# A fused Trainium2 layer: modulation products in four column groups, denser x loads, and the first two projected features moved beside the loads

## The chip, the cores and the metric

The kernel runs on one core of one Trainium2 chip. The metric is device time in microseconds (us); the runs shown are single executions, and the profile is one execution of its own.

## The reference

One layer of a hybrid model in fp32 on 1024 tokens and 256 context tokens of 2048 channels. What matters here is its beginning, an adaptive layer norm and the input projection:

```python
def _modulation(cond, w_ada, b_ada):
    m = jax.nn.silu(cond.astype(F32)) @ w_ada + b_ada
    return jnp.split(m, 3, axis=-1)
...
    shift, scale, gate = _modulation(c, w_ada, b_ada)
    shift_c, scale_c, gate_c = _modulation(c_ctx, w_ada, b_ada)
    h = _layernorm(x, ADALN_EPS) * (1.0 + scale[:, None]) + shift[:, None]
    hc = _layernorm(xc, ADALN_EPS) * (1.0 + scale_c) + shift_c
    s5_u, s5_g, pool_u, pool_g, rkv, rwkv_g, w_codes, a_codes = _split_in(h @ w_in)
    s5_uc, s5_gc, pool_uc, pool_gc, rkv_c, rwkv_gc, w_codes_c, a_codes_c = _split_in(hc @ w_in)
```

Behind it come an S5 scan, a pooling branch, an RWKV recurrence in two directions and an output projection with a last layer norm. `w_in` has 50 blocks of 128 columns, called features here; the last two, 48 and 49, are the codes `w_codes` and `a_codes`.

## The kernel before

`adaln` makes the modulated layer norm. The shift and the scale come from 128 pieces of `w_ada`, each 128 rows by 512 columns (256 KB), which SyncE's queue (SP) loads into a ring of `ARAWS` buffers `araw`; each piece is the moving operand of a product whose stationary operand has two columns, silu of `c` and of `c_ctx`. Sixteen products add up in PSUM (`ada`) to 512 columns of the shift or of the scale. `modulate` copies that row out on ScalarE, turns it into columns by four small products (`misc<-ident,row`), adds the bias on VectorE (`mod`), and after a shift and its scale makes four channel tiles of the activations: VectorE scales and shifts `xT`, ScalarE rounds it (`hi`), VectorE takes the rest (`lo`); the context's tiles go the same way on ScalarE and GpSimd (`hc_hi`, `hc_lo`). Two channel tiles are a slice, and there are eight.

`layernorm` takes a tile of 128 tokens (eight of x, two of the context, 1 MB each): statistics and normalization on VectorE, sixteen transpositions on TensorE, the copies to `xT` shared by ScalarE and VectorE. One x tile is loaded after every seventh piece.

`in_proj` projects feature by feature. `project` runs over the eight slices; of each, two halves of the rounded and rest parts of the weights (`whi`, `wlo`) meet `hi` and `lo` in three products, over 1024 tokens (`pm`, two matmuls) and 256 context tokens (`pc`). SP loads the weights (`wraw`, 128 KB). The order of features is 48, 49, 0 to 3, 24 and so on; 0 to 3 feed S5, and 24 is the first key feature.

TensorE's main stream is written in program order; everything beside it (norm, modulation, `vectors`, `in_parts`, `s5_setup`) is a generator in `Sched`, whose `tick` emits a step when a rough clock of the engines (`Clock`) says that it is due. Each engine and SP's queue then take their instructions in that emitted order. In `project`, as soon as slice 7 is made, `begin` frees the modulation's tiles and starts three jobs: `vectors` (five row vectors loaded into `e`, transposed, then the convolution's 72 rows), `in_parts` (18 rounds that cut `cutraw` into `cuthi`, `cutlo` and store them to `z_lora` or `z_cd`), and `s5_setup` (among others eight rounds of `s5crow`, each transposed on TensorE and stored to `s5c`). After each of the two codes ScalarE takes it out of PSUM into `e0` (one buffer) once `vectors` is over, and stores it to `z_cdraw`. Behind feature 24 `sched.drain()` emits all that is left of the jobs before the next feature.

Of the kernel before, what the change touches and what calls it, by code (L numbers as in the profile page):

```python
# [18 lines left out]
T = 1024  # L19
TC = 256  # L20
# [5 lines left out]
ARAWS = 7  # L26
LINES = 3
RING = 20
# [31 lines left out]
def shape_constants():  # L60
# [5 lines left out]
    c["k_heads"] = hs  # L66
    s = np.arange(64)[:, None]
# [27 lines left out]
class Pace:  # L95
    """Order of emission for engines that take their instructions in turn. It keeps a rough clock of each engine; a job
    says what its next step runs on, for how long, and when its operands are there, and the step is emitted once it
    holds up no engine. Times are in microseconds."""
# [12 lines left out]
    def clocked(self, t, work, share):  # L111
        """When the tensor engine ends what it begins at t: at half its clock after a tick in which it did little."""
# [33 lines left out]
    def offer(self, until):  # L146
        """Emits what is ready: matrix products up to that time, other work not far beyond it."""
# [42 lines left out]
class Slots:  # L190
    """Tiles that jobs take and give back."""
# [44 lines left out]
class Clock:  # L236
    """A rough clock of each engine, kept from the instructions as they are emitted. Times are in microseconds."""
# [9 lines left out]
    def note(self, eng, op, args, kw):  # L247
# [33 lines left out]
class Noted:  # L281
    """An engine, or all of them, whose instructions a clock takes note of."""
# [17 lines left out]
class Rings:  # L300
    """A pool whose tiles the clock takes for the next in the place of an earlier one."""
# [13 lines left out]
    def free(self, tag, bufs, n=1, own=()):  # L315
        """When the next n tiles of that name have been given up, as far as is known; never, while one is kept."""
# [15 lines left out]
class Watched:  # L332
    """A tile context with a clock."""
# [66 lines left out]
def beside(sched, *gens):  # L400
    """Runs gens at the same time, and ends with the last of them."""
# [16 lines left out]
def build(tc, A, out):  # L418
    """A: name -> AP of the inputs and the constants."""
    nc = tc.nc  # L420
    with ExitStack() as ctx:
# [7 lines left out]
        g.kx = scratch("z_kx", (RW, 3, NT))          # k, its unit vector, r  # L429
# [9 lines left out]
        g.cd = scratch("z_cd", (5, 128, 4, 256))         # of each direction the codes in two parts  # L439
# [28 lines left out]
def load_cols_in_steps(tc, A, g, pool, psum, specs, name, ps_tile=None, rows=None):  # L468
    """Vectors cut into rows of 128, turned so that each row is a column."""
# [22 lines left out]
def phase_ab(tc, A, g, const):  # L492
    nc = tc.nc
    with ExitStack() as ctx:
# [8 lines left out]
        with tc.tile_pool(name="araw", bufs=ARAWS) as raws:  # L503
            sched = adaln(tc, A, g, const, hb, psA, ap_, raws, hc_hi, hc_lo)
        g.hc_hi, g.hc_lo = hc_hi, hc_lo
        in_proj(tc, A, g, psA, sched, actx)


def adaln(tc, A, g, const, hb, psA, ap_, raws, hc_hi, hc_lo):
    """The modulated layer norm of both sequences, channels on the partitions, split in two for the products. The main  # L510
    stream is that of the modulation's own products."""
# [13 lines left out]
    def ada_load():  # L525
# [8 lines left out]
        [(rows_of(A["c"], 16), 16), (rows_of(A["c_ctx"], 16), 16), (rows_of(A["b_ada"], 48), 48)], "cv")  # L534
    ada_load()
    x_load()
    g.sil = sil = const.tile([128, 16, 2], FT, name="sil")
# [4 lines left out]
    mod = ap_.tile([128, 16, 2, 2], FT, name="mod")   # [k, shift|scale, c|c_ctx]  # L542
# [40 lines left out]
    def modulate(blk, part, ps):  # L583
        """A block of the modulation as columns; after its second half the block of the activations."""
        row = ap_.tile([2, 512], FT, name="row", tag="row")
        nc.scalar.activation(row, ps[0:2], AF.Copy)
        yield
        pt = psA.tile([128, 512], FT, name="misc", tag="misc", bufs=2)
        for i in range(4):
            nc.tensor.matmul(pt[:, 2 * i:2 * i + 2], row[0:2, i * 128:(i + 1) * 128], g.ident[0:2, 0:2], start=True, stop=True)  # L590
# [10 lines left out]
        while len(hi) < 2 * blk:  # L601
            yield
        for i in (2 * blk, 2 * blk + 1):
# [16 lines left out]

    for j in range(LINES):
# [2019 lines left out]
```

## Time and profile before

| what | value |
|---|---|
| runs | 3113.01, 3110.97, 3103.5 us; median 3110.97 |
| profiled execution | span 3105.6 us (its own time beside the span is not given) |
| TensorE busy | 2901.1 us, 93% |
| VectorE, ScalarE, GpSimd busy | 1992.7, 1024.8, 1030.4 us |
| DMA | 502.56 MB, mean 162 GB/s |

The span is that of one profiled execution, and is read beside the runs, not in their place. TensorE's busy share is a mean over all stages; the change lies in the first 240 us and at one place near 384 us.

### The profile page before, as it was taken

What the parts mean: (1) busy time and instruction counts of PE and PEld (TensorE: products, weight loads), DVE (VectorE), ACT (ScalarE), POOL (GpSimd) and SP (SyncE); (2) the same over time, 40 slices, a digit from 0 to 9 for tenths busy, and PEclk for the clock granted to TensorE, in tenths of its full rate; (3) what the DMA queues carried; (4) which work ended last, traced back from release to release, by engine and by line L of the source; (5) the groups of instructions that cost most, each with busy time, mean ns of one, the idle gap of its engine ahead of it and who ended that gap; (6) DMA issues with size and microseconds to landing.
All of it is one profiled execution on the core that took longest, in us unless ns stands there. A gap on an engine that the chain in (4) does not pass through costs nothing.

```text
span 3105.6 us, 55655 instructions
## 1 busy us (share of the span) xinstructions
PE 2901.1 (93%) x20080; PEld 2350.2 (76%) x20080; DVE 1992.7 (64%) x4464; ACT 1024.8 (33%) x2408; POOL 1030.4 (33%) x1414
## 2 busy tenths in 40 slices
PE   7989999999999999999899779999999999899976
PEld 2268787888888878788677478888888887788855
DVE  5547245545555458898886574766667765774668
ACT  1422223444444443322222223333234333333223
POOL 0103012233333335323541232434344343433516
PEclk9999999999999999999999879899899997996988
DMA  8835634445554555565344655566466665554664
GB/s 279 262 96 157 139 119 156 141 156 168 164 165 150 168 169 158 170 170 160 111 116 133 232 152 157 149 174 176 125 185 175 159 168 151 148 145 114 180 225 153
DMA packets 598828, 502.56 MB, mean 162 GB/s; under 512 B 205358, under 2 KB 519446, under 8 KB 595734
## 3 DMA queue, kind: packets, MB, share of 16 engines
q1 hardware_dynamic: 572792, 453.63, 50.1%
q0 software_dynamic: 6912, 24.12, 2.7%
q10 hardware_dynamic: 18848, 21.24, 2.0%
q8 instruction: 159, 2.61, 0.4%
q14 instruction: 117, 0.96, 0.1%
HBM read 343.77 MB, written 155.07 MB: 161 GB/s over the span
## 4 chain that ended last, share of the span: by engine, by line
PE 71%; DVE 15%; DMA 7%; issue 3%; SPq 2%; ACT 2%; POOL 1%; ACTq 0%; DVEq 0%; POOLq 0%
PE pm L293 28%; PE misc L293 6%; PE gp L1716 4%; PE pc L293 3%; PE ofacc L2371 3%; PE banky L1952 3%; PE ada L293 3%; PE banky L1949 3%; PE banku L1963 2%; PE ofacc L2372 2%; PE ofacc L2373 2%; DVE tmp L1843 2%; PE banky L1982 2%; PE misc L1901 2%; PE misc L1890 2%
## 5 line engine op out<-in xcount | busy, mean ns | idle before, releaser
L293 PE MATMUL pm<-hi,whi 128*128 128x512 f32 x1600 | 509.2, 400 | 7.1 <-ACT whi L293 7.1
L293 PE MATMUL pm<-lo,whi 128*128 128x512 f32 x1600 | 511.5, 401 | 0.0
L293 PE MATMUL pm<-hi,wlo 128*128 128x512 f32 x1600 | 509.0, 399 | 1.6 <-DVE wlo L293 1.6
L293 DVE TENSOR_TENSOR wlo<-wraw,whi 128x256 fp32r<-128x256 f32 x400 | 206.5, 525 | 373.5 <-ACT whi L293 356.5
L293 PEld LDWEIGHTS pm<-hi,whi 128*128 128x128 f32 x1600 | 275.4, 190 | 60.2 <-ACT whi L293 9.4
L293 PEld LDWEIGHTS pm<-hi,wlo 128*128 128x128 f32 x1600 | 274.4, 189 | 54.4 <-DVE wlo L293 2.8
L293 PEld LDWEIGHTS pm<-lo,whi 128*128 128x128 f32 x1600 | 274.0, 190 | 50.3 <-issue 1.8
L293 ACT ACTIVATE whi<-wraw 128x256 fp32r<-128x256 f32 x400 | 160.4, 413 | 400.9 <-DMA wraw<-in_w_in 252.6
L2371 PE MATMUL ofacc<-ofhi,ofyh 128*128 128x256 f32 x768 | 252.6, 329 | 24.3 <-DVE ofev L2388 10.2
L233 POOL TENSOR_TENSOR oflo<-ofw,ofhi 128x256 fp32r<-128x256 f32 x161 | 123.0, 765 | 426.4 <-ACT ofhi L227 308.5
L1989 DVE SCALAR_TENSOR_TENSOR ping<-ping,els,banku 64x64 f32<-64x64 f32 x480 | 134.1, 279 | 177.8 <-PE banku L1975 167.1
L2373 PE MATMUL ofacc<-oflo,ofyh 128*128 128x256 f32 x768 | 227.8, 297 | 1.6 <-POOL oflo L233 1.5
L2372 PE MATMUL ofacc<-ofhi,ofyl 128*128 128x256 f32 x768 | 228.0, 297 | 0.8 <-POOL ofyl L233 0.8
L2371 PEld LDWEIGHTS ofacc<-ofhi,ofyh 128*128 128x128 f32 x768 | 156.8, 204 | 39.1 <-issue 14.3
L1716 PE MATMUL gp<-spread,kq 128*128 128x128 f32 x1152 | 169.9, 295 | 15.5 <-DVE spread L229 6.7
L1716 PEld LDWEIGHTS gp<-spread,kq 128*128 128x128 f32 x1152 | 147.7, 202 | 24.8 <-DVE spread L229 7.0
L2373 PEld LDWEIGHTS ofacc<-oflo,ofyh 128*128 128x128 f32 x768 | 157.6, 205 | 2.7 <-POOL oflo L233 2.3
L2372 PEld LDWEIGHTS ofacc<-ofhi,ofyl 128*128 128x128 f32 x768 | 158.4, 206 | 1.1 <-POOL ofyl L233 1.1
L1843 DVE TENSOR_TENSOR tmp<-af,nn 128x31 f32<-128x31 f32 (+15 forms) x310 | 143.5, 463 | 14.2 <-DMA af<-flat 5.1
L1845 DVE TENSOR_TENSOR nn<-nn,tmp 128x31 f32<-128x31 f32 (+15 forms) x310 | 144.9, 468 | 10.7
L1956 ACT ACTIVATE rhs<-banky 64x256 f32<-64x256 f32 x128 | 48.1, 376 | 271.7 <-PE banky L1952 271.7
L293 ACT ACTIVATE th<-misc,rhalf 128x256 f32<-128x256 f32 x160 | 67.0, 470 | 209.3 <-PE misc L293 191.9
(513 smaller groups left out, 5975.3 us busy)
## 6 DMA issues: line engine op xcount, KB each, us to landing
wraw<-in_w_in SPq DMA_DIRECT2D x400, 128.0 KB, 2.4
z_kq<-kq SPq DMA_DIRECT2D x80, 512.0 KB, 3.9
kq<-z_kq SPq DMA_DIRECT2D x80, 512.0 KB, 4.5
araw<-in_w_ada SPq DMA_DIRECT2D x128, 256.0 KB, 5.0
ofw<-in_w_out SPq DMA_DIRECT2D x192, 128.0 KB, 3.2
part<-ofev SPq DMA_DIRECT2D x96, 256.0 KB, 2.5
cds<-z_cd POOLq DMA_DIRECT2D x40, 512.0 KB, 4.4
agraw<-in_w_ada SPq DMA_DIRECT2D x64, 256.0 KB, 3.0
```

Source lines behind the costliest of these rows:

```text
L233: (nc.vector if eng == "dve" else nc.gpsimd).tensor_tensor(out, a, b, op=op)
L293: r = x(*args, **kw)
L1716: nc.tensor.matmul(gp[:, i], seg.kb[:, i, :], qb[:, i].rearrange("p h t -> p (h t)"), start=True, stop=True)
L1843: nc.vector.tensor_tensor(tv, af[:, q, q + 1:].unsqueeze(2).to_broadcast([128, nt_, nj]), nn[:, q:q + 1, 0:nj].to_broadcast([128, nt_, nj] ...
L1845: nc.vector.tensor_tensor(nn[:, q + 1:, 0:nj], nn[:, q + 1:, 0:nj], tv, op=OP.subtract)
L1890: nc.tensor.matmul(pv[:, j], aq[64:96, c, h * 64 + 32:h * 64 + 64], n1[64:96, j], start=True, stop=True)
L1949: nc.tensor.matmul(yo, seg.qt[:, i], ch.s[d], start=(d == 0), stop=False, skip_group_check=True)
L1952: nc.tensor.matmul(yo[0:64, hs], seg.aq[0:64, i, hs], seg.uv[0:64, ch.uv[d], hs], start=False, stop=False, skip_group_check=True)
L1989: nc.vector.scalar_tensor_tensor(ch.s[d][hs, hs], ch.s[d][hs, hs], seg.el[hs, ch.c[d]:ch.c[d] + 1], b_u[hs, 2 + d, hs], op0=OP.mult, op1=O ...
L2371: nc.tensor.matmul(o, yh[:, sl], whi, start=(first and b == 0), stop=False, skip_group_check=True)
L2372: nc.tensor.matmul(o, yl[:, sl], whi, start=False, stop=False, skip_group_check=True)
L2373: nc.tensor.matmul(o, yh[:, sl], wlo, start=False, stop=last, skip_group_check=True)
```

## The change

Four things are changed in `adaln`, and `in_proj` is fitted to them; the removed docstrings and comments change nothing.

- The stationary operand `sil32` is 32 columns wide (30 of them zero). Products of four consecutive pieces go to PSUM partitions 0, 32, 64 and 96, so to four column groups of the array; `row` is copied out with all 128 partitions, and the turning product uses `fours`, which adds the four groups. `ARAWS` is 5 in the place of 7.
- An x tile is loaded after every second piece.
- In `modulate` the next channel's scale and shift stand ahead of the subtraction.
- Features 48 and 49 (`HEAD`) are projected in `adaln`, slice by slice, as soon as a slice is made: `head_units` holds both `pm` and both `pc` tiles, the weights come over GpSimd's queue into `wraw1`. `pass_time` puts their products where the clock expects the next four pieces to be on their way. `adaln` ends when all sixteen are done; only then `begin` starts the three jobs, and both codes are taken out ahead of feature 0.

```diff
-ARAWS = 7
+ARAWS = 5
+HEAD = (48, 49)
...
+                if out.shape[0] == 32:
+                    cost /= 4
...
+    sil = ap_.tile([128, 16, 32], FT, name="sil32")
+    nc.gpsimd.memset(sil, 0.0)
...
-        row = ap_.tile([2, 512], FT, name="row", tag="row")
-        nc.scalar.activation(row, ps[0:2], AF.Copy)
+        row = ap_.tile([128, 512], FT, name="row", tag="row")
+        nc.scalar.activation(row, ps, AF.Copy)
...
-            nc.tensor.matmul(pt[:, 2 * i:2 * i + 2], row[0:2, i * 128:(i + 1) * 128], g.ident[0:2, 0:2], start=True, stop=True)
+            nc.tensor.matmul(pt[:, 2 * i:2 * i + 2], row[:, i * 128:(i + 1) * 128], fours, start=True, stop=True)
...
-                x, xc = xT[i][:, j], xc_t[:, k]
-                nc.vector.tensor_scalar(x, x, mod[:, k, 1, 0:1], mod[:, k, 0, 0:1], op0=OP.mult, op1=OP.add)
+                xc = xc_t[:, k]
                 nc.scalar.activation(h_hi[:, j], x, AF.Copy)
+                x_next = shifted(k + 1) if k % 4 < 3 else None
                 nc.vector.tensor_tensor(h_lo[:, j], x, h_hi[:, j].bitcast(FT), op=OP.subtract)
+                x = x_next
...
+            nc.gpsimd.dma_start(raw, A["w_in"][0, s * 256:(s + 1) * 256, f * 128:(f + 1) * 128]
+                                .rearrange("(k p) n -> p k n", p=128))
...
+    def head_units():
+
+
+        for n, (s, f) in enumerate(heads):
+            while s not in made:
+                yield None
+            while len(parts) < min(n + 2, len(heads)):
+                w_split()
+            if f not in g.head:
+                g.head[f] = (psA.tile([128, T], FT, name="pm", tag="pm", bufs=2),
+                             psA.tile([128, TC], FT, name="pc", tag="acc", bufs=2))
...
+                    for half in range(2):
+                        nc.tensor.matmul(pm[:, half * 512:(half + 1) * 512], w[:, i, :],
+                                         hs[s][:, i, half * 512:(half + 1) * 512], **st)
+                    nc.tensor.matmul(pc, w[:, i, :], hcs[:, 2 * s + i, :], **st)
+                    yield 0.0
...
+    def pass_time(t):
+
+        clock = tc.clock
+        while True:
+            sched.tick()
+            now = clock.free["tensor"]
+            if now >= t - 0.3:
+                return
+            if not (raw_w and head_step()):
+                clock.free["tensor"] = min(now + 0.25, t)
...
-            if len(loaded) % 7 == 0 and len(x_t) < 10:
+            if len(loaded) % 2 == 0 and len(x_t) < 10:
                 x_load()
         if k == 0:
-            ps = psA.tile([128, 512], FT, name="ada", tag="acc", bufs=2)
-        nc.tensor.matmul(ps[0:2], sil[:, k, :], loaded[n], start=(k == 0), stop=(k == 15))
+            ps = psA.tile([128, 512], FT, name="ada", tag="misc", bufs=2)
+        if k % 4 == 0:
+            if len(normed) == 10 and not raw_w:
+                w_ahead()
+            pass_time(max(tc.clock.written[x.tensor.name][1] for x in loaded[n:n + 4]))
+        c = 32 * (k % 4)
+        nc.tensor.matmul(ps[c:c + 32], sil[:, k, :], loaded[n], start=(k < 4), stop=(k >= 12))
...
+        begin()
         for j, fn in enumerate((AF.Tanh, AF.Copy)):
-            pm, pc = project(48 + j, True)
+            pm, pc = g.head[HEAD[j]]
             while not made.vectors:
                 sched.wait()
```

**TensorE, end of the x transpositions.** `ada<-araw` are the modulation's products, `pm<-ident,x` half of an x tile's transpositions. Before, around the last tile:

```order
L293 MATMUL pm<-ident,x_664 128x128 x8
L293 MATMUL ada<-araw,sil 2x512 x2
L293 MATMUL pm<-ident,x_664 128x128 x8
L293 MATMUL ada<-araw,sil 2x512 x6
L293 MATMUL misc<-ident,row 128x2 x4
L293 MATMUL ada<-araw,sil 2x512 x18
L293 MATMUL misc<-ident,row 128x2 x4
L293 MATMUL ada<-araw,sil 2x512 x13
```

And of the change, with the first unit of feature 48 behind it:

```order
L297 MATMUL pm<-ident,x_373 128x128 x8
L297 MATMUL pm<-ident,x_365 128x128 x8
L297 MATMUL pm<-ident,x_373 128x128 x8
L297 MATMUL ada<-araw,sil_164 32x512 x4
L297 MATMUL misc<-fours,row 128x2 x4
L297 MATMUL ada<-araw,sil_164 32x512 x8
L297 MATMUL pm<-hi_695,whi_725 128x512 x2
L297 MATMUL pc<-hc_hi,whi_725 128x256
```

The last transpositions stood behind 61 pieces and now stand behind 28; the projection began behind all 128 and now begins behind 40.

**ScalarE, behind the last unit.** `e_1634` and `e_1638` are the two codes taken out of PSUM (one buffer), `whi` the split weights of feature 0. Of the change:

```order
L297 ACTIVATE whi_1488<-wraw_1433 128x256
L297 ACTIVATE cuthi<-cutraw 128x256
L297 ACT_TABLE_LOAD
L297 ACTIVATE e_1634<-pm 128x1024
L297 ACTIVATE e_1634<-pc 128x256
L297 DMA z_cdraw<-e_1634 128x1280
L297 ACTIVATE e_1638<-pm 128x1024
L297 ACTIVATE e_1638<-pc 128x256
L297 DMA z_cdraw<-e_1638 128x1280
L297 ACTIVATE whi<-wraw 128x256 x3
```

Before, eight splits of the next feature's weights and three of the cuts lay between the two codes; now nothing does, and the weights of feature 0 stand behind both.

**SP, the drain behind feature 24.** `s5crow` and `s5c` are rounds of S5's factors, `z_cd` and `cutraw` the codes' cuts. Before, from the last weights to the next:

```order
L293 DMA z_cd<-cuthi 64x256
L293 DMA z_cd<-cutlo 64x256
L293 DMA z_cd<-cuthi 64x256
L293 DMA z_cd<-cutlo 64x256
L293 DMA s5c<-s5cc 128x256
L293 DMA s5crow<-in_s_c_re 128x64
L293 DMA s5crow<-in_s_c_im 128x64
L293 DMA s5crow<-in_s_c_re 128x64
L293 DMA s5c<-s5cc 128x256
L293 DMA s5crow<-in_s_c_re 128x64
L293 DMA s5crow<-in_s_c_im 128x64
L293 DMA s5crow<-in_s_c_re 128x64
```

The first part of what stands there now:

```order
L297 DMA s5c<-s5cc 128x256
L297 DMA s5crow<-in_s_c_re 128x64
L297 DMA s5crow<-in_s_c_im 128x64
L297 DMA s5crow<-in_s_c_re 128x64
L297 DMA z_cd<-cuthi 64x256
L297 DMA z_cd<-cutlo 64x256
L297 DMA z_cd<-cuthi 64x256
L297 DMA z_cd<-cutlo 64x256
L297 DMA cutraw<-z_cdraw 128x256
L297 DMA s5c<-s5cc 128x256
L297 DMA s5crow<-in_s_c_re 128x64
L297 DMA s5crow<-in_s_c_im 128x64
```

The rest repeats it: `z_cd` four at a time stands there three times (before once), and 34 loads and stores go out ahead of the last `s5crow` (before 12). On TensorE `misc<-ident,s5crow` is there 14 times in a row and was 10 times.

## Rows read from the trace of the kernel before

**Rows 1.** The page: the span and its instructions.

```profile
span 3105.6 us, 55655 instructions
```

**Rows 2.** Windows: length (us), busy time by engine, granted clock, DMA share, GB/s.

```profile
0.00:167.00 167.00, 147.46 (x473) 46.09 (x473) 88.08 (x156) 46.39 (x97) 10.06 (x16) 0.97 0.79 265
...
120.00:140.00 20.00, 20.00 (x57) 5.02 (x55) 10.82 (x11) 10.46 (x17) 4.11 (x5) 1.00 0.89 292
```

**Rows 3.** The chain that ended last, first 300 us: start, length, work.

```profile
140.40 15.54 PE ada L293 x36
```

**Rows 4.** Groups by form, first 167 us: count | busy, mean ns | idle.

```profile
L293 PE MATMUL ada<-araw,sil 128*2 128x512 f32 x256 | 118.8, 611 | 2.7 <-DMA araw<-in_w_ada 2.7
...
L293 DVE BATCH_NORM_STATS2 bst<-x 128x6 f32<-128x512 f32 x40 | 24.7, 679 | 11.5 <-DMA x<-in_x 11.2 <-DMA x<-in_ctx 0.4
...
L293 DVE TENSOR_SCALAR x<-x,mv 128x2048 f32<-128x2048 f32 x10 | 13.5, 1346 | 0.4
...
L293 DVE TENSOR_TENSOR lo<-xT,hi 128x1024 fp32r<-128x1024 f32 x12 | 14.7, 1225 | 13.5 <-ACT hi L293 13.5
...
L293 DVE COPY xT<-pm 128x256 f32<-128x256 f32 x32 | 13.4, 424 | 20.0 <-ACT xT L293 20.0
...
L293 DVE BATCH_NORM_AGGREGATE mv<-bst 128x2 f32<-128x24 f32 x10 | 2.6, 264 | 0.3
```

**Rows 5.** Loads araw, issue to landing: all, then 120 to 167 us.

```profile
DMA to landing us min/median/max: 2.8/5.0/8.0
...
araw<-in_w_ada SPq DMA_DIRECT2D x45, 256.0 KB, 3.1
```

**Rows 6.** Timeline of PE near 1907 us: start, length, products.

```profile
1907.22 0.45 PE L1975 MATMUL banku<-uv,kbn 128*64 128x64 f32 x8
...
1907.51 0.63 PE L1982 MATMUL banky<-uv,ar 128*64 128x64 f32 x8
...
1908.07 0.68 PE L2040 MATMUL misc<-rhsc,aq 64*64 64x64 f32 x8
```

**Rows 7.** Timeline behind the last modulation product, 167 to 173 us.

```profile
167.41 0.59 ACT L293 ACTIVATE row<-ada 2x512 f32<-2x512 f32 x1 [13.01 <-PE ada L293]
...
172.22 0.81 DVE L293 TENSOR_SCALAR xT<-xT,mod 128x1024 f32<-128x1024 f32 x1
```

**Rows 8.** Timeline 188 to 200 us: the vectors' loads and transposition.

```profile
188.28 0.47 SPq L293 DMA_DIRECT2D heads<-in_k_heads  x1
...
190.40 0.29 SPq L293 DMA_DIRECT2D e<-in_rwkv_r_k  x1
...
192.90 0.32 PE L293 MATMUL misc<-ident,e 56*128 56x56 f32 x1 [7.48 <-DMA e<-in_rwkv_r_k]
```

**Rows 9.** Timeline: a step of products near 201 us, and the second feature's end.

```profile
201.09 0.63 PE L293 MATMUL pm<-hi,wlo 128*128 128x512 f32 x2
...
201.68 0.62 PE L293 MATMUL pm<-hi,whi 128*128 128x512 f32 x2
...
239.20 1.03 ACT L293 ACTIVATE e<-pm 128x1024 f32<-128x1024 f32 x1 [2.03 <-PE pm L293]
```

**Rows 10.** Timeline near 211 us, and z_cdraw's landing (last row).

```profile
211.10 1.03 ACT L293 ACTIVATE e<-pm 128x1024 f32<-128x1024 f32 x1 [6.03 <-PE pm L293]
...
212.43 0.35 ACTq L293 DMA_DIRECT2D z_cdraw<-e  x1
...
DMA to landing us min/median/max: 2.3/2.4/3.2
```

**Rows 11.** Timeline of the stretch behind the fifth feature, 383 to 390 us.

```profile
383.63 0.60 PE L293 MATMUL misc<-ident,s5crow 128*128 128x128 f32 x4
...
386.98 0.38 SPq L293 DMA_DIRECT2D s5crow<-in_s_c_re  x1
...
389.49 0.79 PE L293 MATMUL misc<-ident,s5crow 128*128 128x128 f32 x2 [1.16 <-DMA s5crow<-in_s_c_im]
...
389.94 1.20 PE L293 MATMUL pm<-hi,whi 128*128 128x512 f32 x2
```

More of the change, by code (lines that the diff above doesn't have):

```diff
@@ L66, in shape_constants @@
     c["k_heads"] = hs
+    c["k_fours"] = np.tile(np.eye(32, 2, dtype=np.float32), (4, 1))
     s = np.arange(64)[:, None]
@@ L502, in phase_ab, with adaln @@
         ap_ = actx.enter_context(tc.tile_pool(name="apool", bufs=1, side="right"))
[L503 to L504 removed]
         g.hc_hi, g.hc_lo = hc_hi, hc_lo
[L506 to L509 removed]
+        with tc.tile_pool(name="araw", bufs=ARAWS) as raws, ExitStack() as wctx:
+            sched = adaln(tc, A, g, const, hb, psA, ap_, raws, wctx, hc_hi, hc_lo)
+        assert not sched.q
+        actx.close()
+        in_proj(tc, A, g, psA, sched)
+def adaln(tc, A, g, const, hb, psA, ap_, raws, wctx, hc_hi, hc_lo):
     nc = tc.nc
@@ L602, in modulate, with shifted @@
             yield
+        def shifted(k):
+            x = xT[k // 2][:, k % 2]
+            nc.vector.tensor_scalar(x, x, mod[:, k, 1, 0:1], mod[:, k, 0, 0:1], op0=OP.mult, op1=OP.add)
+            return x
+        x = shifted(4 * blk)
         for i in (2 * blk, 2 * blk + 1):
@@ L619, in modulate, with w_ahead @@
                 yield
+    wp = wctx.enter_context(tc.tile_pool(name="wfirst", bufs=1))
+    heads = [(s, f) for s in range(8) for f in HEAD]
+    raw_w, parts, g.head = [], [], {}
+    def w_ahead():
+        while len(raw_w) < len(heads) and len(raw_w) < len(parts) + 2:
+            s, f = heads[len(raw_w)]
+            raw = wp.tile([128, 2, 128], FT, name="wraw1", tag="wraw1", bufs=2)
+            nc.gpsimd.dma_start(raw, A["w_in"][0, s * 256:(s + 1) * 256, f * 128:(f + 1) * 128]
+                                .rearrange("(k p) n -> p k n", p=128))
+            raw_w.append(raw)
@@ new lines, in w_split @@
+    def w_split():
+        w_ahead()
+        raw = raw_w[len(parts)]
+        whi = wp.tile([128, 2, 128], FR, name="whi1", tag="whi1", bufs=2)
+        wlo = wp.tile([128, 2, 128], FR, name="wlo1", tag="wlo1", bufs=2)
+        nc.scalar.activation(whi, raw, AF.Copy)
+        nc.vector.tensor_tensor(wlo, raw, whi.bitcast(FT), op=OP.subtract)
+        parts.append((whi, wlo))
+        w_ahead()
+    def head_units():
[7 more added lines that the diff above has]
+                             psA.tile([128, TC], FT, name="pc", tag="acc", bufs=2))
+            pm, pc = g.head[f]
+            whi, wlo = parts[n]
+            yield max(tc.clock.written[x.tensor.name][1] for x in (wlo, lo[s], hc_lo))
+            for i in range(2):
+                for m, (w, hs, hcs) in enumerate(((whi, hi, hc_hi), (whi, lo, hc_lo), (wlo, hi, hc_hi))):
+                    st = dict(start=(s == i == m == 0), stop=(s == 7 and i == 1 and m == 2))
+                    for half in range(2):
[3 more added lines that the diff above has]
+                    yield 0.0
@@ new lines, in adaln, with head_step @@
+    units = head_units()
+    ready = [None]
+    def head_step():
+        while ready[0] is None:
+            ready[0] = next(units, "end")
+            if ready[0] is None:
+                return False
+        if ready[0] == "end" or ready[0] > tc.clock.free["tensor"]:
+            return False
+        ready[0] = next(units, "end")
+        return True
+    def pass_time(t):
[7 more added lines that the diff above has]
+                clock.free["tensor"] = min(now + 0.25, t)
@@ L625, in adaln, with in_proj @@
             ada_load()
-            if len(loaded) % 7 == 0 and len(x_t) < 10:
+            if len(loaded) % 2 == 0 and len(x_t) < 10:
                 x_load()
         if k == 0:
-            ps = psA.tile([128, 512], FT, name="ada", tag="acc", bufs=2)
-        nc.tensor.matmul(ps[0:2], sil[:, k, :], loaded[n], start=(k == 0), stop=(k == 15))
+            ps = psA.tile([128, 512], FT, name="ada", tag="misc", bufs=2)
+        if k % 4 == 0:
+            if len(normed) == 10 and not raw_w:
+                w_ahead()
+            pass_time(max(tc.clock.written[x.tensor.name][1] for x in loaded[n:n + 4]))
+        c = 32 * (k % 4)
+        nc.tensor.matmul(ps[c:c + 32], sil[:, k, :], loaded[n], start=(k < 4), stop=(k >= 12))
         if k == 15:
             sched.add(modulate(blk, part, ps), 0)
+    while ready[0] != "end":
         sched.tick()
+        if not head_step() and ready[0] != "end":
+            if sched.q:
+                sched.wait()
+            else:
+                tc.clock.free["tensor"] = ready[0]
     return sched
-def in_proj(tc, A, g, psA, sched, actx):
+def in_proj(tc, A, g, psA, sched):
     nc = tc.nc
@@ L643, in in_proj @@
         kvs, kvts = ExitStack(), ExitStack()
-        feats = ([48, 49] + list(range(0, 4)) + [f for i in range(8) for f in (24 + i, 16 + i, 32 + i)] + list(range(8, 16)) + list(range(4, 8)) + list(range(40, 48)))
+        feats = (list(range(0, 4)) + [f for i in range(8) for f in (24 + i, 16 + i, 32 + i)] + list(range(8, 16)) + list(range(4, 8)) + list(range(40, 48)))
         todo = [(f, s) for f in feats for s in range(8)]
@@ L674, in project @@
             for s in range(8):
-                while s not in g.made:
-                    sched.wait()
-                if len(g.made) == 8 and not made.begun:
-                    begin()
                 whi, wlo = w_load(f, s)
@@ L695, in in_proj @@
         made.k = made.r = 0
-        made.busy = made.held = made.begun = made.vectors = False
+        made.busy = made.held = made.vectors = False
         def begin():
-            made.begun = True
-            actx.close()
             sched.add(vectors())
@@ L1148, in ada_gate @@
             yield raw,
[L1149 removed]
+            sc = g.sil[:, k:k + 1]
             if k == 0:
```

8 lines of the change are left out of this document (5 added, 3 removed).

## The prediction

> **What bounds the kernel now.** I read the windows first, then the chain that ended last, then groups by form, and last the timelines of the places that the change moves. The profiled span is 3105.6 us [rows 1]; no other time of that execution is given, and the median of the three runs shown, 3110.97 us, is 5.4 us above it. I work in differences and apply the sum to the median.
>
> The change touches the first 240 us and one place near 384 us. In the first 167 us the modulation's weights and x are loaded, and TensorE is busy for 147 of them; from 120 to 140 us it has no idle time at full clock while the DMA engines carry 292 GB/s [rows 2]. The chain there is nothing but modulation products, 36 in a row in 15.54 us [rows 3]. A record of that group counts twice per product (256 for 128 pieces, each a 256 KB slice of w_ada), so one piece takes 15.54/18 = 0.863 us [rows 3, 4]. Hence TensorE paces the end of the loads. Behind it codes 48 and 49 are projected, ending at about 239.1 us [rows 9]; a wait of 7.48 us for vectors lies between [rows 8].
>
> **Part 1, the column groups.** Four consecutive pieces now go to four groups of 32 columns. No row of before shows four groups. The nearest are two runs of eight small products: those that alternate between two column halves start 0.29 us before the next run, those that all lie in one half 0.56 us before it (1907.51 − 1907.22 and 1908.07 − 1907.51) [rows 6]. Two groups thus overlap almost wholly. Per four pieces the bounds are 3.45 us (no overlap), 1.73 (two at a time) and 0.86 (all four). I take 0.86 to 1.73, being nearest to that pair; either way TensorE is no longer the pace, so the choice does not enter the sum.
>
> The Trainium skill, "TensorEngine Tiling (Array Packing)", section Key Properties, states that a change of tiling mode drains TensorE, which speaks against groups of four between full-width products. Rows 6 pass from products on 128 rows and 64 columns to products on 64 rows and 64 columns, and the second run starts 0.07 us before the first one's modelled end: no hole of 0.1 us. Some 45 changes at that bound would be 4 us, an estimate, in slack beside the loads.
>
> What is late next is the load. There are now five buffers, not seven. A buffer's round is landing, wait, product: landing took 3.1 us in the undisturbed part, 2.8 at least, 5.0 in the middle of all [rows 5]. With 3.1 + about 1.0 (four nearly parallel products) + 0.15 for release, a round is 4.27 us, over five buffers 0.854 us per piece; by the lower bound 0.79, by the median 1.23. So the products become four times cheaper and the pace hardly changes. That is the first reason why the gain is small.
>
> **Part 2, x per two pieces.** All ten x tiles are then asked for by piece 16 instead of piece 56. The layer norm becomes VectorE's: per tile four statistics (4 × 0.679), an aggregate 0.264 and some 0.3 of small ones, the normalization 1.346, four copies (4 × 0.424), 6.3 us [rows 4]; 63 us for ten, from some 8 us on, with a few us for gaps: the last transpositions at about 75 us (72 to 84). In the order the last of them stand behind piece 28, and five more lie loaded.
>
> **Part 3, codes beside the loads.** Sixteen units (18 products, 6 steps of 0.59 us, 3.5 us) stand between pieces [rows 9]. After 75 us come four pieces, the second modulation row, eight pieces, the first slices' channels and the first weights, about 11 us (12 pieces less the five loaded, 7 × 0.854 = 6 us, and some 5 for row and first slice). Then 88 pieces and 12 units: 12 × 3.5 = 42 us of TensorE, and 88 × 0.854 = 75 us of loads, partly one beside the other, since in a unit only five buffers can fill. By the order a block of 32 pieces has four units, three of whose groups of four wait hidden, and 20 pieces that wait bare: 4 × 3.5 + 20 × 0.854 + about 4 = 35 us; two blocks and the last 24 pieces make 97 us (82 to 105). The last product ends at 75 + 11 + 97 = 183 us, 16 later than before. The head weights go over GpSimd's queue, which costs SP no issue; their 2 MB take 7 us of the loads' 290 GB/s [rows 2], inside the 97.
>
> **Part 4, the tail.** The last modulation row, its transposition and the sum took from 167.41 to 172.22 us, with other work between [rows 7]; 2.6 us when nothing stands between. Behind it slices 6 and 7 are made. VectorE's order now has the next channel's scaling ahead of the subtraction, so a channel costs VectorE's own two, 1.23 for the subtraction [rows 4] and 0.8 to 1.2 for the scaling [rows 7], about 2.3 us, with the rounding beside them; four units (14.2 us) then take 17.8 us, the wait for slice 6 included. The codes end at 183 + 20.4 = 203.5 us.
>
> **Part 5, what the codes' projection used to cover.** `begin` (vectors, factors, S5's setup) now stands behind the last unit. Its wait for vectors was 7.48 us bare already [rows 8]; the rest hid under 28 us of feature 48. Now: five vector loads issued in 2.4 us (188.28 to 190.69), landing 2.2 (to 192.90), so the first transposition is at +4.7 us [rows 8]; the convolution's load waits for it and for the copy out of PSUM (0.5), is issued (0.5), lands 2.2 later and is turned at +8.2; only then may ScalarE take the first code out (1.03 + 0.38 us), from +8.6 to +10.0; its store lands 2.4 us behind its issue, and the second code waits for the buffer [rows 10], +12.5 to +13.9. Feature 0's weights are split behind both on ScalarE: +14.7, first product +14.8, and 1.6 us more at the lower clock. Feature 0 is in effect at 203.5 + 16.4 = 220 us against 239.1: 19 us gained.
>
> **Part 6, the drain behind feature 24.** There all setup still open is emitted before TensorE goes on: 6.3 us in before, from 383.63 to 389.94 [rows 11]. The setup's jobs now begin behind feature 49, not inside feature 48, so seven rounds of s5crow and three of z_cd are left instead of five and one. SP issues 34 loads and stores ahead of the last round at about 0.42 us (0.38 for one of them [rows 11]), 14.3 us, of which 1 lies beside feature 24; with landing and transposition 15.1 us. Lost: 9 us. Bounds: 6 us if SP is ahead of TensorE, 13 if it is behind already.
>
> **Sum:** 19 − 9 = 10 us gained, 3110.97 − 10 = 3101 us.
>
> **The rivals.** (a) *The groups do not overlap* (other side). For it: no row shows four; against it: rows 6. Then some 96 pieces × 0.863 and 12 units × 3.5 follow one another on TensorE from 75 us on: 83 + 42 + 5, last product at 205 us, codes at 226, feature 0 at 242, 3 us lost, with the drain 12: 3123 us. The point from which it decides is 2.8 us per four pieces: above that TensorE is the pace again.
> (b) *The loads keep pace with the units*: a piece lands in 2.8 us and the five buffers refill under each unit, so the 88 pieces take 75 us instead of 97. For it: 2.8 is seen [rows 5]; against it: with x or weights beside them pieces took 5. Last product at 161 us, feature 0 at 198: 41 − 9 = 32 us gained, 3079 us. The Trainium skill's "DMA: Bandwidth & Descriptors", section Specifications, gives about 358 GB/s of HBM per core; by it the 25 MB left at 86 us would take 70 us, the same case. The trace averaged 265 [rows 2].
> (c) *The gain is given back*: VectorE's stage ends at 84 us, or pieces land in 3.6 us, and the wait of part 5 and the drain stay. Each moves the last product by 8 to 10 us: 3109 to 3113 us, no change.
> (d) *SP's queue is late beyond the drain*: feature 3 has 56 issues in the new order, which at about 0.45 us fill its 28 us; if weights are late behind them, 5 to 8 us more: 3107 us.
>
> **How the numbers follow.** Forecast 0.47 (3096 to 3106), (a) 0.12, (b) 0.18, (c) 0.15, (d) 0.08. What a measurement of this kernel can tell from no change is 0.3%, 9.3 us; so 3101.6 and 3120.3 are the limits. Faster: (b) and 0.27 of the forecast's, 0.45; slower: (a) and a tail of (c), 0.18; the same: 0.37. The range, 3076 to 3123 us, takes in (b) and (a) to their middles.
>
> **What would show it.** Right: no 36 products in a row in the chain, pieces start to start near 0.85 us with TensorE idle between, the last transposition of x near 75 us, the last modulation product at 178 to 188, codes ending near 203, an idle stretch of about 15 us before feature 0 with the vectors' loads, ScalarE and z_cdraw in it, and one of 12 to 17 us behind feature 24 with SP issuing throughout. Wrong: four pieces in 3.4 us of busy TensorE (a); last product before 170 us (b); idle TensorE inside feature 3 (d). The step I trust least is the 97 us.

## The result and the profile after

The changed kernel ran at 3120.53 us in the median of 19 runs (3112.07 to 3149.56), the kernel before at 3100.72 us in 19 (3089.45 to 3117.96). The ratio is 1.0065, 95% interval 1.0043 to 1.0087: slower by 0.65%, some 20 us, where 10 us were forecast as a gain. The time itself lies inside the range that was given, 3076 to 3123 us; the direction does not agree. The three runs of before that the forecast was added to (median 3110.97) lay 10 us above the median of 19, so the times below are read as ratios and as places on the span. The profiled execution took 3119.32 us, its span 3117.5.

The windows of the changed kernel (stretch and length, busy time by engine, granted clock, DMA share, GB/s), to be read beside [rows 2]:

```profile
20.00:40.00 20.00, 12.62 (x69) 7.94 (x68) 14.93 (x30) 5.48 (x16) 0.00 (x0) 0.91 0.98 380
40.00:60.00 20.00, 10.44 (x55) 8.62 (x54) 15.50 (x35) 3.99 (x12) 0.00 (x0) 0.67 0.25 89
20.00:60.00 40.00, 23.07 (x122) 16.57 (x121) 30.43 (x65) 9.47 (x28) 0.00 (x0) 0.79 0.61 235
60.00:80.00 20.00, 11.64 (x66) 6.42 (x64) 14.02 (x28) 4.53 (x14) 0.00 (x0) 0.76 0.32 105
...
100.00:120.00 20.00, 19.36 (x102) 11.48 (x100) 3.27 (x7) 3.09 (x7) 3.92 (x5) 1.00 0.56 184
120.00:140.00 20.00, 15.05 (x52) 5.07 (x52) 9.19 (x10) 8.55 (x14) 4.44 (x5) 1.00 0.80 262
140.00:160.00 20.00, 19.60 (x103) 11.76 (x101) 2.02 (x6) 1.74 (x4) 3.16 (x4) 1.00 0.59 188
```

The x tiles come in one burst, 380 GB/s from 20 to 40 us. Behind it, from 40 to 80 us, the memory does little (89 and 105 GB/s): the five buffers are full, and their products stand in TensorE's order behind transpositions that wait for VectorE (7.33 us at 77.03, in the timeline below). From 100 us on a stretch rich in units (184, 188 GB/s) takes turns with one poor in them (262); the kernel before carried 292 from 120 to 140 us [rows 2]. Groups by form, first 220 us (busy us, mean ns | idle before, and what ended it), beside [rows 4]:

```profile
L297 PE MATMUL ada<-araw,sil 128*32 128x512 f32 x256 | 73.6, 647 | 17.6 <-DMA araw<-in_w_ada 17.4
L297 DVE COPY xT<-pm 128x256 f32<-128x256 f32 x32 | 13.3, 423 | 15.6 <-ACT xT L297 15.5
```

The products' busy time fell from 118.8 to 73.6 us, and their idle time rose from 2.7 to 17.6, for the loads. VectorE's copies wait 15.5 us for ScalarE's. The tile `araw` (what PE's queue of weight loads waited for, and issue to landing), beside [rows 5]:

```profile
L297 PE MATMUL ada<-araw,sil x256: 592/617/1062, 10.6 to 206.2; 128*32 128x512 f32 x128
...
  DMA araw<-in_w_ada: 70.2, 74
...
DMA to landing us min/median/max: 2.7/3.4/8.9
```

TensorE's products and weight loads of this group waited 70.2 us for loads, in 74 places (in the kernel before 9.7 us, in 10). TensorE's timeline (start, length, work): transpositions of x with a group of four pieces (eight records) between them, the last transposition, the first unit, a group of four pieces inside units, two modulation rows that stand 32 pieces apart, and the last products:

```profile
58.32 3.65 PE L297 MATMUL pm<-ident,x 128*128 128x128 f32 x16 [1.41 <-DVE mod L297]
61.90 1.91 PE L297 MATMUL ada<-araw,sil 128*32 128x512 f32 x8
63.74 1.97 PE L297 MATMUL pm<-ident,x 128*128 128x128 f32 x16
...
77.03 1.94 PE L297 MATMUL pm<-ident,x 128*128 128x128 f32 x8 [7.33 <-DVE mv L297]
...
83.76 1.06 PE L297 MATMUL pm<-ident,x 128*128 128x128 f32 x8 [1.03 <-DVE xT L297]
...
97.19 0.73 PE L297 MATMUL pm<-hi,whi 128*128 128x512 f32 x2 [1.13 <-ACT whi L297]
...
100.10 0.28 PE L297 MATMUL pc<-hc_lo,whi 128*128 128x256 f32 x1
100.31 1.07 PE L297 MATMUL ada<-araw,sil 128*32 128x512 f32 x8
101.31 0.73 PE L297 MATMUL pm<-hi,wlo 128*128 128x512 f32 x2
101.87 0.28 PE L297 MATMUL pc<-hc_hi,wlo 128*128 128x256 f32 x1
101.99 0.62 PE L297 MATMUL pm<-hi,whi 128*128 128x512 f32 x2
...
129.28 1.05 PE L297 MATMUL misc<-fours,row 128*128 128x2 f32 x8 [0.75 <-ACT row L297]
...
168.44 1.05 PE L297 MATMUL misc<-fours,row 128*128 128x2 f32 x8 [0.75 <-ACT row L297]
...
202.94 3.85 PE L297 MATMUL ada<-araw,sil 128*32 128x512 f32 x10 [0.17 <-DMA araw<-in_w_ada]
```

The last products end at 206.8 us, against 167.3 before. Behind the last unit, which ends at 226.6, the timeline of all engines, beside [rows 8, 10]:

```profile
226.61 0.33 SPq L297 DMA_DIRECT2D heads<-in_k_heads  x1
...
230.31 0.24 PE L297 MATMUL misc<-ident,e 56*128 56x56 f32 x1 [3.73 <-DMA e<-in_rwkv_r_k]
...
234.80 0.35 PE L297 MATMUL misc<-ident,e 72*128 72x72 f32 x1 [1.46 <-DMA e<-in_conv_rkv]
...
236.18 1.02 ACT L297 ACTIVATE e<-pm 128x1024 f32<-128x1024 f32 x1
...
241.40 1.02 ACT L297 ACTIVATE e<-pm 128x1024 f32<-128x1024 f32 x1 [3.93 <-DMA z_cdraw<-e]
...
243.63 1.22 PE L297 MATMUL pm<-hi,whi 128*128 128x512 f32 x2 [8.47 <-ACT whi L297]
```

And behind feature 24, on TensorE, beside [rows 11]:

```profile
361.03 1.22 PE L297 MATMUL pm<-hi,whi 128*128 128x512 f32 x2 [2.55 <-ACT whi L297]
...
390.83 0.60 PE L297 MATMUL misc<-ident,s5crow 128*128 128x128 f32 x4
...
398.34 0.66 PE L297 MATMUL misc<-ident,s5crow 128*128 128x128 f32 x2 [5.43 <-DMA s5crow<-in_s_c_im]
...
409.77 1.20 PE L297 MATMUL pm<-hi,whi 128*128 128x512 f32 x2
```

Feature 0 starts 4.5 us later than before (243.63 against 239.1), feature 24 ends 7.2 us later (390.83 against 383.63), after a wait of 2.55 us for its weights, and the feature behind the drain starts 19.8 us later (409.77 against 389.94 [rows 11]). That is the whole loss: from there on nothing is gained or lost that the ratio would show.

What holds the drain is told by the chain that ended last (start, length, work). One of its rounds, the first of two alike:

```profile
393.56 2.36 DMA cutraw<-z_cdraw
...
396.02 0.42 ACT cuthi L297
...
396.47 0.43 DVE cutlo L297
396.89 0.47 DVE s5cc L297 x2
...
398.25 0.59 SPq L297
...
398.89 2.36 DMA cutraw<-z_cdraw
```

The rounds of `s5crow` and the rounds of the cuts are tied together. `s5cc`, which takes `s5crow` out of PSUM, stands in VectorE's order behind `cutlo`; that waits for ScalarE and for the load of `cutraw`; and SP issues this load behind the stores of the cut before. Such a round takes 5.3 us.

### The profile page after: what moved, and what is told of

It reads as the page before. It is cut to its first block, busy times and chain, and to the rows that moved or that the text cites. A ratio compares the mean times of both kernels' runs of the same rounds, so it can differ in the third digit from the quotient of the medians.

```text
span 3117.5 us, 55667 instructions
## 1 busy us (share of the span) xinstructions
PE 2860.8 (92%) x20080; PEld 2345.6 (75%) x20080; DVE 1989.0 (64%) x4464; ACT 1024.6 (33%) x2409; POOL 1046.6 (34%) x1431
## 4 chain that ended last, share of the span: by engine, by line
PE 72%; DVE 14%; DMA 7%; issue 3%; ACT 2%; SPq 2%; POOL 0%; ACTq 0%; DVEq 0%; POOLq 0%
PE pm L297 30%; PE misc L297 6%; PE gp L1812 4%; PE pc L297 4%; PE ofacc L2467 3%; PE banky L2048 3%; PE banky L2045 3%; PE banku L2059 2%; PE ofacc L2468 2%; PE ofacc L2469 2%; PE banky L2078 2%; DVE tmp L1939 2%; PE misc L1997 2%; PE misc L1986 2%; SPq L297 2%
## 5 line engine op out<-in xcount | busy, mean ns | idle before, releaser
L297 PE MATMUL pm<-hi,whi 128*128 128x512 f32 x1600 | 511.0, 401 | 16.9 <-ACT whi L297 14.7
L2467 PEld LDWEIGHTS ofacc<-ofhi,ofyh 128*128 128x128 f32 x768 | 155.8, 203 | 40.4 <-issue 15.5
```

Source lines behind the costliest of these rows:

```text
L297: r = x(*args, **kw)
L2467: nc.tensor.matmul(o, yh[:, sl], whi, start=(first and b == 0), stop=False, skip_group_check=True)
```

## The experiments

The start of the first product behind the drain is the landmark. In every kernel its distance from 389.94, over 3100 us, lies within the interval of the ratio, so one profile is taken to divide the time by place. A place is not exact: up to their last pieces the changed kernel, codes_first and pool_stores are the same code, and these start at 206.2, 204.8 and 210.0 us. A difference of some 5 us between two kernels is therefore weak evidence unless their ratios part too. Each ratio is against 19 to 29 executions of the kernel before. Drain is from the first `s5crow` behind feature 24 (or the feature's end) to the landmark.

| kernel | last piece starts, us | drain, us | landmark, us | ratio to before, 95% interval |
|---|---|---|---|---|
| before | 166.7 | 6.3 | 389.94 | 1 |
| changed | 206.2 | 18.9 | 409.77 | 1.0065 (1.0043 to 1.0087) |
| codes_first | 204.8 | 36 | 413.04 | 1.0106 (1.0062 to 1.015) |
| no_heads | 181.8 | 6.3 | 403.07 | 1.0041 (1.0016 to 1.0065) |
| no_heads_seven | 163.2 | 6.4 | 384.77 | 0.9984 (0.995 to 1.0017) |
| groups_x7 | 158.4 | 6.2 | 378.88 | 0.9959 (0.9938 to 0.998) |
| one_column | 172.4 | 6.3 | 393.31 | 1.0006 (0.998 to 1.0032) |
| four | 215.5 | 18.8 | 418.97 | 1.008 (1.0051 to 1.0109) |
| pool_stores | 210.0 | 16.9 | 407.68 | 1.0058 (1.003 to 1.0086) |
| heads_six | 194.8 | 22.8 | 402.51 | 1.0034 (1.0006 to 1.0062) |
| one_head | 197.5 | 18.9 | 407.70 | 1.0044 (1.0021 to 1.0067) |
| x4_eight | 150.6 | 6.3 | 372.98 | 0.9939 (0.9915 to 0.9962) |
| x5_eight | 145.8 | 6.2 | 366.66 | 0.9936 (0.9905 to 0.9967) |

The theory before the experiments was that the five buffers and the units hold the loads up, and that the setup has lost its cover. The rivals were that the groups or x per two pieces are the loss, and that the setup's time is only moved.

**codes_first**

```diff
         made.codes = False
-        begin()
         for j, fn in enumerate((AF.Tanh, AF.Copy)):
             pm, pc = g.head[HEAD[j]]
-            while not made.vectors:
-                sched.wait()
             o = ev("e0")
...
         made.codes = True
+        begin()
```

> The changed kernel with one edit: both codes are taken out of PSUM and stored before the setup jobs begin, so that ScalarE does not wait for the vectors. Theory (the time behind the last unit is the wait for vectors that nothing covers any more): the idle stretch of 17 us before feature 0 shrinks to about 7, some 10 us less, ratio to the kernel before about 1.003. Rival (the setup is only moved, and its time comes back at the drain behind feature 24, 19 us there now): the drain grows by as much, ratio stays near 1.0065.

Feature 0 starts at 233.49, 10.1 us earlier than in the changed kernel, as the theory says. But TensorE's timeline behind feature 24 has this:

```profile
376.59 0.38 PE L297 MATMUL misc<-ident,s5crow 128*128 128x128 f32 x2
380.85 0.99 PE L297 MATMUL misc<-ident,s5crow 128*128 128x128 f32 x2 [3.88 <-DMA s5crow<-in_s_c_im]
...
408.00 0.66 PE L297 MATMUL misc<-ident,s5crow 128*128 128x128 f32 x2 [4.48 <-DVE s5cc L297]
...
413.04 1.20 PE L297 MATMUL pm<-hi,whi 128*128 128x512 f32 x2
```

Feature 24 ends at 377 us, and the drain takes 36 us. The rival holds: the theory's ratio of 1.003 lies below the interval, and the 13.8 us by which feature 24 ends earlier are gone at the landmark. The setup begins later still: its vectors are turned on TensorE at 253.43 us, behind products of feature 0, not at 230.31, and the drain is 17 us longer. That every microsecond of a later begin is paid there is a reading of these places; that more than was saved is lost is not shown, since the intervals of this run and of the changed kernel overlap.

**no_heads and no_heads_seven**, the same edit with five buffers and with seven; the projection beside the loads is taken out, and the stationary tile moves to a pool that ends with the pieces:

```diff
+        feats = ([48, 49] + list(range(0, 4))
...
+                if len(g.made) == 8 and not made.begun:
+                    begin()
...
-            pm, pc = g.head[HEAD[j]]
+            pm, pc = project(48 + j, True)
...
-ARAWS = 5
+ARAWS = 7
```

> The changed kernel without the projection of features 48 and 49 beside the loads: they are projected in in_proj again, where the setup begins inside feature 48; the four column groups, x per two pieces and five buffers stay. Theory (the units hold the loads up, since only five buffers can fill beside a unit, and the setup loses its cover): the 88 last pieces run at the pace of five buffers, about 0.86 us each, last product near 171 us against 206, feature 0 near 243 us as now, but the drain is back at 6 to 7 us: ratio about 1.001 to 1.003. Rival (the projection beside the loads is a gain, and the loss comes from x or from the groups): ratio above 1.0065.

> As the run without the projection beside the loads, with seven buffers for pieces. Theory (five buffers set the pace of the loads): 0.75 to 0.79 us a piece behind the x stage, last product 8 us or more earlier than with five, ratio about 0.996 to 0.999. Rival (the memory sets the pace, not the buffers): no difference from five beyond 2 us.

With five buffers the last piece comes at 181.8, 11 us later than expected; the ratio, 1.0041, lies above the expected band, and its interval reaches to the changed kernel's. So by its place most of the loss, 13.1 of 19.8 us, is there without any unit. The pace was wrong, and TensorE's timeline gives it: sixteen pieces lie between these two rows.

```profile
151.61 1.05 PE L297 MATMUL misc<-fours,row 128*128 128x2 f32 x8 [0.75 <-ACT row L297]
...
167.33 1.05 PE L297 MATMUL misc<-fours,row 128*128 128x2 f32 x8 [0.69 <-ACT row L297]
```

15.72/16 = 0.98 us a piece with five buffers and no unit beside them, not 0.854; the landing of these loads is 3.6 us in the median (3.3 to 3.8), not 3.1. With seven the same loads are faster. The windows with seven come first, then those with five:

```profile
100.00:120.00 20.00, 17.78 (x58) 4.06 (x56) 9.07 (x10) 8.58 (x15) 4.47 (x4) 1.00 0.94 311
120.00:140.00 20.00, 18.28 (x70) 5.09 (x69) 3.13 (x6) 2.44 (x4) 1.29 (x2) 1.00 0.91 320
```

```profile
100.00:120.00 20.00, 15.54 (x49) 3.62 (x49) 0.34 (x2) 1.19 (x2) 0.00 (x0) 1.00 0.79 263
120.00:140.00 20.00, 16.49 (x57) 4.29 (x56) 9.47 (x11) 8.22 (x13) 4.91 (x4) 0.91 0.75 251
```

311 and 320 GB/s against 263 and 251. Over 64 pieces (from the row at 96.98 us to that at 152.23) seven buffers take 0.86 us a piece, slower than the 0.75 to 0.79 expected; five take 1.00 (103.53 to 167.33). Two buffers are worth 18.3 us at the landmark, and here the ratios differ as well, 0.9984 against 1.0041, though their ends touch (1.0017 and 1.0016). It is the largest term on this way from kernel to kernel.

**groups_x7 and one_column.** The first is no_heads_seven with an x tile per seven pieces, the second the same with one column group (`row` then has 32 partitions):

```diff
-            if len(loaded) % 2 == 0 and len(x_t) < 10:
+            if len(loaded) % 7 == 0 and len(x_t) < 10:
...
-        c = 32 * (k % 4)
-        nc.tensor.matmul(ps[c:c + 32], sil[:, k, :], loaded[n], start=(k < 4), stop=(k >= 12))
+        nc.tensor.matmul(ps[0:32], sil[:, k, :], loaded[n], start=(k == 0), stop=(k == 15))
```

> The four column groups with seven buffers and x per seven pieces, without the projection beside the loads: part 1 of the change and VectorE's order alone. Theory (in the kernel before TensorE paced the pieces, and x per two pieces only trades their order): last product near 155 us against 167, ratio about 0.996. Rival (the loads pace it as well, x arriving late): last product near 165, ratio 0.999 to 1.000.

> The kernel of groups_x7 (seven buffers, x per seven pieces, codes projected in in_proj) with all products in one column group, in the same order. Theory (the overlap of the four groups is what groups_x7 gained): TensorE takes 0.86 us a piece again, last product near 167 us against 159, ratio to the kernel before 0.999 to 1.002. Rival (it gained by VectorE's order or by the emission): ratio near 0.996.

The groups gain: 0.9959, and in one column, with VectorE's order kept, the gain is gone (1.0006). So it is the column groups and not VectorE's order. The last pieces come 3 us later than expected in groups_x7 (158.4) and 5 in one_column (172.4). The windows of one_column show TensorE as the pace again:

```profile
120.00:140.00 20.00, 20.00 (x54) 5.72 (x52) 10.04 (x11) 10.08 (x16) 4.18 (x6) 1.00 0.86 289
```

Against no_heads_seven x per seven pieces is 5.9 us better at the landmark. That x per two pieces was a loss too is likely but not shown: the intervals overlap (0.9938 to 0.998 against 0.995 to 1.0017), and places scatter by 5 us.

**four and heads_six**, the changed kernel with four and with six buffers. For six, the stationary tile is packed and one raw buffer of the head weights goes:

```diff
-    sil = ap_.tile([128, 16, 32], FT, name="sil32")
+    sil = ap_.tile([128, 62], FT, name="sil32")
...
-        nc.tensor.matmul(ps[c:c + 32], sil[:, k, :], loaded[n], start=(k < 4), stop=(k >= 12))
+        nc.tensor.matmul(ps[c:c + 32], sil[:, 2 * k:2 * k + 32], loaded[n], start=(k < 4), stop=(k >= 12))
...
-            raw = wp.tile([128, 2, 128], FT, name="wraw1", tag="wraw1", bufs=2)
+            raw = wp.tile([128, 2, 128], FT, name="wraw1", tag="wraw1", bufs=1)
...
-ARAWS = 5
+ARAWS = 6
```

> The changed kernel with four buffers for pieces in the place of five. Theory (in the changed kernel too the number of buffers sets the pace of the loads): about 1.25 us a piece where it is bare, 15 to 20 us longer, ratio 1.011 to 1.013. Rival (units and x set it): within 4 us of the changed kernel, ratio 1.006 to 1.008.

> The changed kernel with six buffers for pieces; the room comes from a narrower stationary tile (neighbouring columns shared, the surplus rows of PSUM are weighted with zero) and one buffer in the place of two for the raw head weights. Theory (the buffers that the head weights displaced are the loss): four to five buffers brought the last product 9 us forward, six bring it another 6 to 9, ratio 1.003 to 1.005. Rival (the units hold the loads whatever the buffers, or the single raw buffer costs as much): ratio 1.006 or above.

From four to five the last piece comes 9.3 us earlier, from five to six 11.4. Four costs less than the 15 to 20 us expected, and its ratio, 1.008, is at the upper end of what the rival gave; that part of the loads lies under units that take their time anyway would explain it, but was not tried. Six has the expected ratio. Of its 11.4 us 7.3 are left at the landmark, since the drain grows to 22.8. The units do not make the buffers unimportant.

**pool_stores**, the changed kernel with one queue changed:

```diff
-                                nc.sync.dma_start(g.cd[i[1], r:r + 64, 2 * i[0] + d], (hi, lo)[h][own])
+                                nc.gpsimd.dma_start(g.cd[i[1], r:r + 64, 2 * i[0] + d], (hi, lo)[h][own])
```

> The changed kernel with the 40 stores of the cut codes (z_cd) issued by GpSimd's queue, not SP's. Theory (the drain behind feature 24 is SP's backlog of issues): the drain falls from 19 us to 11 to 13, and the wait of 2.5 us before feature 24 goes, ratio 1.003 to 1.004. Rival (the drain is the chain of the s5crow rounds, each waiting for the one before: 8 rounds of 1.9 us): the drain stays at 15 us or more, ratio 1.005 or above.

The wait ahead of feature 24 is gone (feature 0 starts 4.1 us later than in the changed kernel, feature 24 ends at the same 390.8), but the drain still takes 16.9 us. So SP's share that could be taken away was 2 us of the drain; the rounds hold the rest, since each still waits for the landing of its loads and for the stores that free its buffers. The intervals of this run and of the changed kernel overlap almost wholly, so the ratio alone is inconclusive here, and the profiled span (3129.0) is high among this kernel's runs; only places within this execution are compared. TensorE's timeline:

```profile
394.97 0.58 PE L297 MATMUL misc<-ident,s5crow 128*128 128x128 f32 x2 [2.67 <-DMA s5crow<-in_s_c_im]
397.77 0.66 PE L297 MATMUL misc<-ident,s5crow 128*128 128x128 f32 x2 [2.23 <-DVE s5cc L297]
...
402.52 0.66 PE L297 MATMUL misc<-ident,s5crow 128*128 128x128 f32 x2 [4.09 <-DVE s5cc L297]
```

**one_head**, feature 48 alone beside the loads:

```diff
-HEAD = (48, 49)
+HEAD = (48,)
...
-        feats = (list(range(0, 4))
+        feats = ([49] + list(range(0, 4))
...
+        second = project(49, True)
         for j, fn in enumerate((AF.Tanh, AF.Copy)):
-            pm, pc = g.head[HEAD[j]]
+            pm, pc = second if j else g.head[48]
```

> The changed kernel with feature 48 alone projected beside the loads; the setup begins behind it and feature 49 is projected in in_proj, so that its 28 us cover the vectors. Theory (uncovered setup and two features of units are both too much): the idle 17 us before feature 0 nearly gone, units half, last product near 194 us, the drain still 14 to 17 us, ratio 1.001 to 1.004. Rival (whatever is saved ahead of feature 0 comes back at the drain, as in codes_first): ratio 1.0065 or above.

The idle stretch is gone, the last piece comes at 197.5 (expected 194), and the drain stays at 18.9: 1.0044, just above the expected band. With one feature the last piece comes 15.7 us later than with none (181.8), with the second another 8.7, so the first costs the loads more; the drain of 18.9 us comes with either.

**x4_eight and x5_eight**, groups_x7 with eight buffers and x per four or five pieces:

> The kernel of groups_x7 with eight buffers and an x tile per four pieces. Theory (buffers set the pace up to what the memory gives, and x between the two rates is best): last product near 153 us, ratio 0.993 to 0.995. Rival (at seven buffers the memory sets the pace): as groups_x7, ratio 0.996, last product within 3 us of 158.

> The kernel of x4_eight with an x tile per five pieces. Theory (four is near the best between two and seven): last product 151 to 156 us, ratio 0.994 to 0.996. Rival (x later is better still with eight buffers): ratio below 0.993.

```profile
60.00:80.00 20.00, 14.18 (x86) 8.55 (x88) 14.86 (x32) 5.24 (x16) 0.00 (x0) 0.91 0.76 259
...
100.00:120.00 20.00, 18.00 (x57) 4.18 (x57) 8.13 (x10) 8.83 (x14) 3.59 (x4) 1.00 0.98 341
```

Both beat the kernel before and the changed kernel: 0.9939, as expected, and 0.9936, which their intervals do not tell apart. That four is the best distance is thus not shown; x5_eight has the earlier last piece, 145.8, where 151 to 156 was expected. Against groups_x7 (0.9959) the intervals overlap. The rows are of x5_eight: the memory carries 341 GB/s from 100 to 120 us, and 259 from 60 to 80 where the changed kernel carried 105.

## Why the prediction was wrong

- *The sum by experiments.* At the landmark the four groups (with VectorE's order and seven buffers) gain 11.1 us (389.94 to 378.88), x per two pieces costs 5.9 (384.77), five buffers in the place of seven 18.3 (403.07), and the projection beside the loads 6.7 (409.77). That is 19.8 us lost, against 20 by the medians. The terms hold for this order of steps; in another order they would divide otherwise, and 5.9 and 6.7 are hardly more than the scatter of a place.
- *Where the forecast went astray.* It gave 10 us gained, the landmark shows 19.8 lost. Of these 30 us 11.2 arose ahead of the first unit (97.2 us, not 86), 12.6 from there to the last product (109.6 us, not 97), and some 6 behind it.
- *Part 1, the groups:* right. Four pieces take 1.0 us from start to start inside units (100.31 to 101.31), near the bound of 0.86 taken for all four; rival (a) is out. The Trainium skill's "TensorEngine Tiling (Array Packing)", section Key Properties, has TensorE drain at each change of mode. Here the group starts 0.21 us behind the start of the `pc` ahead of it (100.10 to 100.31), where a full-width product starts 0.12 behind (101.87 to 101.99): 0.09 us more, and no hole of 0.1 us.
- *Part 1, the pace of five buffers:* this is the step that failed. "0.854 us per piece" took the landing of 3.1 us from a stretch in which TensorE, not the buffers, made the pace, and a sum of parts for the rest of the round. Measured in no_heads: 0.98 bare, a round of 4.9 us, of which the landing is 3.6. The sentence that the pace hardly changes hid the comparison that mattered: with seven buffers and free TensorE the same loads run at 311 to 320 GB/s, so the buffers gave away what the groups had won. The upper bound of the estimate, 1.23, was in the text and not used. No run shows the 0.15 us for release.
- *Part 2, VectorE's stage:* mis-sized. The last transposition began at 83.76, not 75 (the range went to 84). The sum of durations left out the idle time in the very row it quoted: 20.0 us of VectorE's copies waiting for ScalarE's [rows 4]; they wait 15.5 after. At the lower clock (0.76 to 0.79 granted, from 20 to 80 us) sixteen transpositions took 3.65 us (at 58.32), at full clock 1.97 (at 63.74).
- *Part 3:* two blocks of 32 pieces took 39.2 and 39.1 us, expected 35. By the prediction's own count 20 pieces of a block wait bare; at 0.98 in the place of 0.854 these make 2.5 of the 4 us, and the rest is open.
- *Parts 4 and 5:* right. From the last product to the last unit 19.8 us (20.4 expected), from there to the first product of feature 0 17.0 (14.8 expected), in the order of waits that was written: vectors, convolution, first code, store, second code, weights. Of the 2.2 us too many, 1.0 had arisen at the first code (236.18), and 1.3 more at the second (241.40), which waited 3.93 us for the store.
- *Part 6:* the mechanism right, the size 18.9 us in the place of 15.1, so 12.6 us lost in the place of 9. SP's last 30 issues up to the last load of `s5crow` start 0.57 us apart (391.14 to 407.75), not 0.42. And the reason given was only part of it: with the stores taken from SP in pool_stores 16.9 us stay, held by the chain of rounds, in which loads and stores of the cuts must land before the next goes on. That the drain comes from the later setup and not from the units beside the loads is what codes_first and one_head speak for.
- *Rival (d)* held with its 2.55 us ahead of feature 24, less than the 5 to 8 given. Rival (b), loads that keep pace with the units, did not happen (last product at 206.8, not 161; with six buffers the last piece started at 194.8), and units with seven buffers were not tried. Rival (c) named both conditions rightly, VectorE's stage to 84 us and a landing of 3.6, but as alternatives, each worth 8 to 10 us; both came.
- *Luck:* that 3120.53 us lies inside the range is luck. Its upper end was set by rival (a), whose mechanism did not happen, and the time was added to a median 10 us above that of the 19 runs.

Left open: why x per two pieces costs 5.9 us at seven buffers, if it does. The last piece is 4.8 us later, and the memory is at 158 GB/s there from 60 to 80 us against 258 in groups_x7; that the burst of x fills the ring while products wait behind transpositions was read from the order and the windows, not tried by itself.

## What to carry to other kernels

When an engine that made the pace gets faster, the next pace can be the ring of buffers, as here: take the landing time from a stretch that is limited by the ring, and count a buffer that is given up for room as a change of its own. Work that begins later because it lost its place in the order must be followed to the place where everything open is waited for; here it was paid there. And a stage is not the sum of its engine's durations when the row beside them shows whom they wait for.

## What was not expected of the hardware

Taking work off TensorE lowered its granted clock: 0.79 and 0.76 in the windows from 20 to 80 us, nearly half of that time at the lower of its two levels (1.2 GHz), where the kernel before had 0.96 from 20 to 60. TensorE had been busy for 23.07 of these 40 us, before for 34.39. The windows of groups_x7 and one_column, which differ in the column groups alone, show the same, 0.84 against 0.96:

```profile
20.00:60.00 40.00, 28.66 (x144) 14.19 (x144) 27.05 (x57) 8.32 (x25) 0.00 (x0) 0.84 0.81 281
20.00:60.00 40.00, 33.58 (x137) 15.19 (x136) 23.08 (x50) 7.58 (x22) 0.00 (x0) 0.96 0.76 261
```

In the changed kernel a group of four pieces took 1.84 us there (61.90 to 63.74) against 1.0 at full clock, and sixteen transpositions 3.65 against 1.97. In groups_x7 a transposition of x took 330 ns in the mean from 20 to 80 us, in one_column 289. So making the products beside the loads cheaper made the transpositions slower.

The memory gave more than rival (b) reckoned with. With x tiles of 1 MB and pieces of 256 KB under way together the changed kernel moved 380 GB/s from 20 to 40 us, above the 358 of that rival; pieces and weights behind the x stage came to 341 at most, with eight buffers.
